# Both ends of a two-layer encoder kernel: parameter load, first weight pieces, clock warm-up, root table and stores

## The chip, the cores and the metric

The kernel runs on one core of one Trainium2 chip. The metric is the device time of one execution in microseconds (us). A core has TensorE (matmul, "PE" in the profile, its weight loads "PEld"), VectorE ("DVE"), ScalarE ("ACT"), GpSimd ("POOL") and SyncE ("SP"), which here only issues DMAs. A DMA is issued by an engine's queue (SPq, ACTq, POOLq) and carried out by 16 DMA engines that all queues share.

## The reference

`reference()` runs two layers over x, 512 tokens of 1024 channels. Cut to what matters:

```python
for l in range(DEPTH):                      # DEPTH = 2
    x = x + 0.5 * swiglu_ffn(rmsnorm(x, ffn1_norm[l]), ffn1_w_in[l], ffn1_w_out[l])
    h = rmsnorm(x, mix_norm[l])
    ...                                     # RWKV-7, gated linear attention, memory attention
    x = x + merged @ w_out[l]
    x = x + 0.5 * swiglu_ffn(rmsnorm(x, ffn2_norm[l]), ffn2_w_in[l], ffn2_w_out[l])
return rmsnorm(x, final_norm)

def rmsnorm(x, g):
    y = x * rsqrt(mean(x * x, axis=-1) + 1e-6)
    return y * g

def swiglu_ffn(h, w_in, w_out):             # 1024 -> 2 x 2816 -> 1024
    gate, up = split(h @ w_in, 2)
    return (silu(gate) * up) @ w_out
```

The change touches the start of the first layer's `ffn1` and the last `ffn2` together with the final `rmsnorm`.

## The kernel before

x is held transposed in eight tiles `x[k]` of 128 channels by 512 tokens (`T`). All products are float32 made from two-part operands: `split` writes a rounded part `hi` (ScalarE, a copy) and the remainder `lo` (VectorE, a subtraction), and `mm3` adds hi·hi, hi·lo and lo·hi in PSUM.

*Order of the work.* The program is recorded first: every call becomes an `Op` in a `Recorder`, with its dependences worked out from the areas that it reads and writes. `cost` gives every operation a duration, `run` plays the list through five engines and one DMA pipe, `urgency` works out backwards how late each may start, and `plan` repeats this six times and keeps the order with the earliest end. `issue` then emits that order, which is fixed on each engine. TensorE prefers the order of recording; the other engines take what is most urgent among what is ready.

*Front.* `setup` loads the parameter tile `par` (124 columns, among them the norm gains) through GpSimd's queue, runs `NWARM` = 9 products of a column of ones, whose result nobody reads, and loads x through SyncE. `ffn` then makes `xr` (the two parts of x times the norm gain, `raw_in`: tiles xrh and xrl; the eighth k is called xr), starts the sum of squares for the norm (`rstd`, tiles sq and sqa, a product with ones, a root, a reciprocal and a product with the unit matrix that spreads the result over the partitions), and computes the first four hidden tiles with plain products: `whole(j)`. The norm's factor `rs` is applied only to the result, so these products need not wait for it. `whole` loads the 1 MB of tile j in two pieces of 512 KB (k = 0 to 3 and 4 to 7; gate and up side by side), splits each, and makes 2 x 3 matmuls for every k. The split pieces `whi` and `wlo` have two buffers each, the raw piece `wraw` three. The other hidden tiles go through `seven`, a scheme of seven half-size products for four, with operands made in `blocks_in`; its loads use the ring `q`, and some of them are accumulated by GpSimd's DMAs. The memory's norm is interleaved into the first layer's down products (`aside`) and borrows two buffers of `q`.

*End.* The hidden tiles of the last `ffn` come in three blocks, each followed by its four down products (o = 0 to 3, two tiles of x each). Before the last block's down products a one-element Sqrt is recorded (`self.root`), which loads Sqrt's table into ScalarE; it reads slot 0 of the last pair of hidden tiles, written when the pair's even tile is done. `finish` squares x[0] to x[5] whole and sums them, then takes the two halves of the tokens in turn (the upper first): squares of x[6] and x[7], sums over the partitions by products with ones (in ps_f and ps_c), root, reciprocal, spreading by the unit matrix `cst`, and then for every k one VectorE product with the gain and the factor and one store of 128 KB on SyncE's queue: 16 stores.

Of the kernel before, what the change touches and what calls it, by code (L numbers as in the profile page):

```python
# [19 lines left out]
P = 128  # L20
T = 512
D = 1024
KD = 8
# [7 lines left out]
NWARM = 9  # L31
# [253 lines left out]
class Recorder:  # L285
# [65 lines left out]
    def cost(self, o, ins, outs, a, k):  # L351
# [32 lines left out]
        elif o.engine == "scalar":  # L384
# [11 lines left out]
        else:  # L396
# [3 lines left out]
            o.busy, o.took = max(440, o.pipe), o.pipe + 1450  # L400
# [33 lines left out]
    def run(self, late):  # L434
# [42 lines left out]
        while events:  # L477
# [22 lines left out]
            for e in touched:  # L500
# [21 lines left out]
                if o.pipe is not None:  # L522
                    dma = max(t + 400, dma) + o.pipe
                    o.took = dma - t + (1050 if e == "sync" else 2550)
# [15 lines left out]
    def urgency(self, order):  # L540
# [7 lines left out]
        for o in reversed(order):  # L548
            t = late.get(o, math.inf)
            for q in o.next:  # L550
                g = self.lag(o, q)
                took = o.took if o.pipe is None else o.pipe + (1450 if o.engine == "sync" else 2950)
# [41 lines left out]
class Net:  # L594
# [34 lines left out]
    def setup(self):  # L629
# [3 lines left out]
        nc.gpsimd.dma_start(out=self.par, in_=I["par"][0])  # L633
# [6 lines left out]
        self.x = [self.keep.tile([P, T], F32, name=f"x{k}", tag=f"x{k}") for k in range(KD)]  # L640
# [331 lines left out]
    def ffn(self, w_in, w_out, norm, aside=None, last=False):  # L972
# [3 lines left out]
        with ExitStack() as ctx:  # L976
# [7 lines left out]
            def whole(j):  # L984
                src = w_in[j]
                pp = self.big(), self.small("i")
                w = [self.piece(pool, self.load(src, c, c + 2 * T).rearrange("p (c t) -> p c t", c=2)) for c in (0, 2 * T)]
                for k in range(KD):
                    ks = slice(k % 4 * P, k % 4 * P + P)
                    for ps, (a, b) in zip(pp, w[k // 4]):  # L990
                        self.mm3(ps, (a[:, ks], b[:, ks]), xs[k], k == 0, k == KD - 1)
# [61 lines left out]
            def jobs():  # L1053
                for b, (j0, j1) in enumerate(BLOCKS):
# [4 lines left out]
                    if b == len(BLOCKS) - 1 and last:  # L1059
                        self.root = self.nrm.tile([P, 4], F32, name="rt", tag="rt", bufs=2)  # L1060
                        nc.scalar.activation(self.root[:, 0:1], Ms[b][n - 1][0][:, 0, 0:1].bitcast(F32), AF.Sqrt,
                                             bias=self.eps[:, 0:1], scale=0.0)
                    for o in range(4):
                        if aside is not None and b == 0 and o == 1:
                            aside(pool)
                        nc.part = "down"
# [724 lines left out]
    def finish(self, out):  # L1791

        nc = self.nc
        acc, sq = (self.keep.tile([P, 2, T], F32, name="sqa", tag=t) for t in ("kT", "vm"))
        rt = self.root
        for k in range(KD - 2):
            nc.scalar.activation(acc[:, int(k > 0)], self.x[k], AF.Square)
            if k:
                nc.vector.tensor_tensor(acc[:, 0], acc[:, 0], acc[:, 1], ALU.add)
        for i, hs in enumerate(HALVES[::-1]):  # L1800
            for k in range(2):
                nc.scalar.activation(sq[:, k, hs], self.x[KD - 2 + k][:, hs], AF.Square)
# [11 lines left out]
            for k in range(KD):  # L1814
# [79 lines left out]
```

## Time and profile before

| | |
|---|---|
| median of 3 runs | 2542.26 us (2540.98 to 2543.71) |
| profiled execution | 2542.58 us, of which the span is 2540.7 |
| busy, share of the span | PE 99%, PEld 89%, DVE 83%, ACT 58%, POOL 10% |
| chain that ended last | PE 86%, DVE 7%, DMA 3%, issue 2%, ACT 1% |
| TensorE without work, 0 to 50 us | 3.5 us |
| TensorE without work, 100 to 150 us | 4.0 us |
| DMA over the span | 358 MB, 141 GB/s on average |

"Busy" counts from the start of an engine's instruction to its end. The chain is followed back from the last instruction to what released it. In a row of the timeline the first two numbers are start and length in us, then come engine, line, operation, out<-in, and in square brackets how long the engine had been idle and what ended that. Nearly everything has line 316, since the calls are replayed from there, so instructions are told apart by their tiles. A row of a window table has the window, its length, the busy time and count for PE, PEld, DVE, ACT and POOL, the granted TensorE clock (1.00 is full speed), the busy share of the DMA engines and their GB/s. "DMA to landing" is the time from a DMA's issue until its data are there.

### The profile page before, as it was taken

Reading aid. Unit: us, or ns where it says so; the run is one execution under the profiler, and the core shown is the slowest. Engines: PE = TensorE matmul, PEld = TensorE weight load, DVE = VectorE, ACT = ScalarE, POOL = GpSimd, SP = SyncE. Lnnn points to the kernel's source line nnn. Section 1 sums busy time; section 2 is a strip of 40 time slices with the busy share of each in tenths; the row PEclk is TensorE's granted clock in tenths of the full one; section 3 lists DMA queues with packets and bytes.
Section 4 is the critical chain, followed back from the end, with each engine's and each line's share of the span. In section 5 each row is a group of like instructions: output and inputs, shape, how many; then the busy total and the mean of one; then the engine's idle time right before and its main releaser. Section 6 shows DMA issues by size and latency. Waiting matters only on the chain.

```text
span 2540.7 us, 47191 instructions
## 1 busy us (share of the span) xinstructions
PE 2506.8 (99%) x17630; PEld 2270.9 (89%) x17630; DVE 2099.7 (83%) x4218; ACT 1467.9 (58%) x2660; POOL 241.4 (10%) x363
## 2 busy tenths in 40 slices
PE   9999999999999999999999999999999999999998
PEld 8999988888888899999989999877887788899998
DVE  7988885778888689888889888766878877898877
ACT  6665666664544456565655656674745444565655
POOL 1111100000000001211101111000000000011110
PEclk9999999999999999999999999999999999999999
DMA  6787762322222556877558776523222225468773
GB/s 194 186 200 185 171 189 81 118 79 69 69 83 74 144 156 153 206 188 185 145 132 202 188 188 168 170 87 103 83 69 88 67 77 170 134 165 208 187 177 100
DMA packets 162884, 358.02 MB, mean 141 GB/s; under 512 B 18224, under 2 KB 37104, under 8 KB 162656
## 3 DMA queue, kind: packets, MB, share of 16 engines
q1 hardware_dynamic: 125760, 289.92, 37.0%
q0 software_dynamic: 36896, 65.09, 16.4%
q8 instruction: 139, 2.28, 0.4%
q14 instruction: 89, 0.73, 0.1%
HBM read 342.88 MB, written 12.06 MB: 140 GB/s over the span
## 4 chain that ended last, share of the span: by engine, by line
PE 86%; DVE 7%; DMA 3%; issue 2%; ACT 1%; SPq 0%; DVEq 0%; ACTq 0%; POOLq 0%
PE ps_b L316 41%; PE ps_i L316 25%; PE ps_f L316 10%; PE ps_c L316 9%; PE ps_y L316 2%; DVE wlo L316 1%; DMA q<-in_ffn_out_dram 1%; DVE x L316 1%; DMA mt<-in_mem_dram 1%; DVE lo L316 0%; ACT whi L316 0%; DMA q<-in_w_out_dram 0%; DMA wraw<-in_ffn_in_dram 0%; DMA wraw<-in_w_out_dram 0%; ACT hi L316 0%
## 5 line engine op out<-in xcount | busy, mean ns | idle before, releaser
L316 ACT ACTIVATE hi<-q 128x512 fp32r<-128x512 f32 (+3 forms) x384 | 289.2, 756 | 206.1 <-PE ps_i L316 67.6
L316 DVE TENSOR_TENSOR lo<-q,hi 128x512 fp32r<-128x512 f32 (+3 forms) x384 | 323.0, 843 | 44.6 <-ACT hi L316 44.3
L316 PE MATMUL ps_b<-xhi,whi 128*128 128x512 f32 (+1 forms) x880 | 353.7, 402 | 0.2 <-DVE rk_r L316 0.2
L316 PE MATMUL ps_b<-xlo,whi 128*128 128x512 f32 (+1 forms) x880 | 352.9, 401 | 0.1
L316 PE MATMUL ps_b<-xhi,wlo 128*128 128x512 f32 x864 | 347.1, 402 | 0.4 <-DVE wlo L316 0.3
L316 DVE TENSOR_TENSOR wlo<-wraw,whi 128x1024 fp32r<-128x1024 f32 (+1 forms) x172 | 183.8, 1069 | 74.7 <-ACT whi L316 70.5
L316 DVE TENSOR_TENSOR lo<-wraw,hi 128x1024 fp32r<-128x1024 f32 (+1 forms) x160 | 191.6, 1197 | 59.7 <-ACT hi L316 58.7
L316 ACT ACTIVATE whi<-wraw 128x1024 fp32r<-128x1024 f32 (+1 forms) x174 | 161.7, 929 | 129.6 <-PE ps_b L316 99.5
L316 ACT ACTIVATE hi<-wraw 128x1024 fp32r<-128x1024 f32 (+1 forms) x160 | 165.8, 1036 | 106.6 <-PE ps_i L316 41.2
L316 PEld LDWEIGHTS ps_b<-xlo,whi 128*128 128x128 f32 (+1 forms) x880 | 164.1, 187 | 35.6 <-DVE xlo L316 2.5
L316 PEld LDWEIGHTS ps_b<-xhi,whi 128*128 128x128 f32 (+1 forms) x880 | 164.4, 187 | 33.6 <-issue 1.2
L316 PEld LDWEIGHTS ps_b<-xhi,wlo 128*128 128x128 f32 x864 | 162.7, 188 | 32.5 <-DVE wlo L316 1.9
L316 PE MATMUL ps_i<-mh,hi 128*128 128x256 f32 x628 | 157.3, 283 | 8.0 <-DVE x L316 6.0
L316 PE MATMUL ps_i<-ml,hi 128*128 128x256 f32 x624 | 155.0, 281 | 0.0
L316 PE MATMUL ps_b<-xhi,hi 128*128 128x256 f32 x576 | 144.4, 283 | 0.0
L316 PE MATMUL ps_b<-xlo,hi 128*128 128x256 f32 x576 | 144.3, 283 | 0.0
L316 PEld LDWEIGHTS ps_i<-mh,hi 128*128 128x128 f32 x628 | 119.0, 190 | 10.1 <-ACT hi L316 3.8
L316 PEld LDWEIGHTS ps_i<-ml,hi 128*128 128x128 f32 x624 | 118.1, 190 | 0.0
L316 PEld LDWEIGHTS ps_b<-xhi,hi 128*128 128x128 f32 x576 | 110.5, 192 | 0.2
L316 PEld LDWEIGHTS ps_b<-xlo,hi 128*128 128x128 f32 x576 | 110.4, 192 | 0.1
L316 ACT ACT_TABLE_LOAD x73 | 93.7, 1283 | 15.9 <-DVE gc L316 10.8
L316 PE MATMUL ps_b<-ml,hi 128*128 128x256 f32 x416 | 101.9, 278 | 0.0
(415 smaller groups left out, 7011.2 us busy)
## 6 DMA issues: line engine op xcount, KB each, us to landing
wraw<-in_w_main_dram SPq DMA_DIRECT2D x108, 512.0 KB, 3.6
wraw<-in_ffn_in_dram SPq DMA_DIRECT2D x104, 512.0 KB, 4.5
q<-in_ffn_in_dram SPq DMA_DIRECT2D x144, 256.0 KB, 4.5
q<-in_ffn_in_dram POOLq DMA_DIRECT2D x72, 256.0 KB, 5.8
d<-in_ffn_in_dram SPq DMA_DIRECT2D x72, 256.0 KB, 4.3
wraw<-in_ffn_in_dram POOLq DMA_DIRECT2D x72, 256.0 KB, 5.4
wraw<-in_ffn_out_dram SPq DMA_DIRECT2D x32, 512.0 KB, 4.4
q<-in_ffn_out_dram SPq DMA_DIRECT2D x64, 256.0 KB, 3.7
```

The costliest lines, as they stand in the source:

```text
L316: return getattr(getattr(self.tc.nc, engine), what)(*(f(v) for v in a), **{n: f(v) for n, v in k.items()})
```

## The change

- `setup`: `par` of layer 0 is loaded by ScalarE's queue, and 12 products of ones run instead of 9. The planner learns the cost of a DMA on ScalarE's queue.
- `x` becomes one tile `xs` of 128 x 8 x 512, of which x[k] are views.
- `whole(0)` of the first `ffn` loads four pieces of two k (256 KB) instead of two pieces of four k; all other hidden tiles keep pieces of four k. Load, split and products are now recorded piece by piece.
- The one-element Sqrt is recorded between the down products o = 1 and o = 2 of the last block and reads slot 6 of the last pair, written with the last odd tile's upper half, after its Silu.
- `finish`: x[0] to x[5] are multiplied by the gain early, after their squares. In each half, x[0..2] and x[3..5] then take one product with the factor each (three tiles at once) and one store of 384 KB, on SyncE's and on ScalarE's queue; x[6] and x[7] take the former product and a store of 128 KB each, one on each queue: 8 stores.

```diff
-NWARM = 9
+NWARM = 12
...
-        nc.gpsimd.dma_start(out=self.par, in_=I["par"][0])
+        nc.scalar.dma_start(out=self.par, in_=I["par"][0])
...
-        self.x = [self.keep.tile([P, T], F32, name=f"x{k}", tag=f"x{k}") for k in range(KD)]
+        self.xs = self.keep.tile([P, KD, T], F32, name="x", tag="x")
+        self.x = [self.xs[:, k, :] for k in range(KD)]
...
-                w = [self.piece(pool, self.load(src, c, c + 2 * T).rearrange("p (c t) -> p c t", c=2)) for c in (0, 2 * T)]
-                for k in range(KD):
-                    ks = slice(k % 4 * P, k % 4 * P + P)
-                    for ps, (a, b) in zip(pp, w[k // 4]):
-                        self.mm3(ps, (a[:, ks], b[:, ks]), xs[k], k == 0, k == KD - 1)
+                n = fine if j == 0 else 4
+                wide = src.rearrange("p (h c t) -> p h c t", h=2, c=2)
+                for k0 in range(0, KD, n):
+                    raw = self.wp.tile([P, 2, n * P], F32, name="wraw", tag="wraw", bufs=3)
+                    t0 = k0 % 4 * P
+                    nc.sync.dma_start(out=raw, in_=wide[:, k0 // 4, :, t0:t0 + n * P])
+                    w = self.piece(pool, raw)
+                    for k in range(k0, k0 + n):
+                        ks = slice((k - k0) * P, (k - k0 + 1) * P)
+                        for ps, (a, b) in zip(pp, w):
+                            self.mm3(ps, (a[:, ks], b[:, ks]), xs[k], k == 0, k == KD - 1)
...
-                    if b == len(BLOCKS) - 1 and last:
-                        self.root = self.nrm.tile([P, 4], F32, name="rt", tag="rt", bufs=2)
-                        nc.scalar.activation(self.root[:, 0:1], Ms[b][n - 1][0][:, 0, 0:1].bitcast(F32), AF.Sqrt,
-                                             bias=self.eps[:, 0:1], scale=0.0)
                     for o in range(4):
...
+                        if b == len(BLOCKS) - 1 and last and o == 2:
+                            self.root = self.nrm.tile([P, 4], F32, name="rt", tag="rt", bufs=2)
+                            nc.scalar.activation(self.root[:, 0:1], Ms[b][n - 1][0][:, 6, 0:1].bitcast(F32), AF.Sqrt,
+                                                 bias=self.eps[:, 0:1], scale=0.0)
...
-        for k in range(KD - 2):
+        early = KD - 2
+        for k in range(early):
             nc.scalar.activation(acc[:, int(k > 0)], self.x[k], AF.Square)
             if k:
                 nc.vector.tensor_tensor(acc[:, 0], acc[:, 0], acc[:, 1], ALU.add)
+            nc.vector.tensor_scalar(self.x[k], self.x[k], self.pcol("final_norm", k), None, ALU.mult)
+        rows = out.rearrange("(k p) t -> p k t", p=P)
...
-            for k in range(KD):
-                nc.vector.scalar_tensor_tensor(self.x[k][:, hs], self.x[k][:, hs], self.pcol("final_norm", k), ps[:, :H],
+            for k0, k1, queue in ((0, 3, nc.sync), (3, early, nc.scalar)):
+                nc.vector.tensor_tensor(x[:, k0:k1, hs], x[:, k0:k1, hs],
+                                        ps[:, :H].unsqueeze(1).to_broadcast([P, k1 - k0, H]), ALU.mult)
+                queue.dma_start(out=rows[:, k0:k1, hs], in_=x[:, k0:k1, hs])
+            for k, queue in ((KD - 2, nc.sync), (KD - 1, nc.scalar)):
+                nc.vector.scalar_tensor_tensor(x[:, k, hs], x[:, k, hs], self.pcol("final_norm", k), ps[:, :H],
                                                ALU.mult, ALU.mult)
-                nc.sync.dma_start(out=out[k * P:(k + 1) * P, hs], in_=self.x[k][:, hs])
+                queue.dma_start(out=rows[:, k, hs], in_=x[:, k, hs])
...
-            self.ffn(self.I["ffn1_in"][l], self.I["ffn1_out"][l], "ffn1_norm", self.layer_params)
+            self.ffn(self.I["ffn1_in"][l], self.I["ffn1_out"][l], "ffn1_norm", self.layer_params, fine=4 if l else 2)
```

More of the change, by code (lines that the diff above doesn't have):

```diff
@@ L383, in cost @@
             o.busy = max(o.took - 80, 60)
-        elif o.engine == "scalar":
+        elif o.engine == "scalar" and o.what != "dma_start":
             n = out.n
@@ L399, in cost @@
             o.pipe = size / 230
-            o.busy, o.took = max(440, o.pipe), o.pipe + 1450
+            o.busy, o.took = 440 if o.engine == "scalar" else max(440, o.pipe), o.pipe + 1450
     HOP, SLACK = 34, 60
@@ L523, in run @@
                     dma = max(t + 400, dma) + o.pipe
-                    o.took = dma - t + (1050 if e == "sync" else 2550)
+                    o.took = dma - t + (2550 if e == "gpsimd" else 1050)
                 if e == "tensor":
@@ L551, in urgency @@
                 g = self.lag(o, q)
-                took = o.took if o.pipe is None else o.pipe + (1450 if o.engine == "sync" else 2950)
+                took = o.took if o.pipe is None else o.pipe + (2950 if o.engine == "gpsimd" else 1450)
                 t = min(t, late[q] - (o.busy if g is None else took + g))
@@ L970, in outputs, with ffn @@
         return evict
-    def ffn(self, w_in, w_out, norm, aside=None, last=False):
+    def ffn(self, w_in, w_out, norm, aside=None, last=False, fine=4):
         nc, l = self.nc, self.l
@@ L1791, in finish @@
     def finish(self, out):
-        nc = self.nc
+        nc, x = self.nc, self.xs
         acc, sq = (self.keep.tile([P, 2, T], F32, name="sqa", tag=t) for t in ("kT", "vm"))
         rt = self.root
-        for k in range(KD - 2):
+        early = KD - 2
+        for k in range(early):
             nc.scalar.activation(acc[:, int(k > 0)], self.x[k], AF.Square)
@@ L1799, in finish @@
                 nc.vector.tensor_tensor(acc[:, 0], acc[:, 0], acc[:, 1], ALU.add)
+            nc.vector.tensor_scalar(self.x[k], self.x[k], self.pcol("final_norm", k), None, ALU.mult)
+        rows = out.rearrange("(k p) t -> p k t", p=P)
         for i, hs in enumerate(HALVES[::-1]):
-            for k in range(2):
-                nc.scalar.activation(sq[:, k, hs], self.x[KD - 2 + k][:, hs], AF.Square)
+            for k in range(early, KD):
+                nc.scalar.activation(sq[:, k - early, hs], self.x[k][:, hs], AF.Square)
             ps, r = self.small("fc"[i]), rt[:, 2 * i:2 * i + 2]
```

## The prediction, made before the changed kernel was run

> **What bounds the kernel now.** I read the page's head and its chain first, then the two ends of the span in order of time, then windows.
>
> ```profile
> span 2540.7 us, 47191 instructions
> ...
> PE 2506.8 (99%) x17630; PEld 2270.9 (89%) x17630; DVE 2099.7 (83%) x4218; ACT 1467.9 (58%) x2660; POOL 241.4 (10%) x363
> ...
> PE 86%; DVE 7%; DMA 3%; issue 2%; ACT 1%; SPq 0%; DVEq 0%; ACTq 0%; POOLq 0%
> ```
>
> TensorE is busy for 99% of the span and carries 86% of the chain that ended last. A change that leaves the matmuls alone can win only where TensorE stands still or runs slowly: at the front, at the end, or in one of the few waits between. The front, in order of time (start, length, engine):
>
> ```profile
> 0.94 4.21 PE L316 MATMUL ps_y<-one 128*128 128x128 f32 x18 [0.94 <-DVE eps L316]
> 1.20 1.37 SPq L316 DMA_DIRECT2D x<-in_x_dram  x3
> 1.29 0.70 POOL L316 DMA_DIRECT2D par<-in_par_dram  x1 [0.83 <-POOLq L1876]
> ...
> 5.19 1.06 ACT L316 ACTIVATE hi<-wraw 128x1024 fp32r<-128x1024 f32 x1 [3.15 <-DMA wraw<-in_ffn_in_dram]
> ...
> 6.28 1.23 DVE L316 TENSOR_TENSOR lo<-wraw,hi 128x1024 fp32r<-128x1024 f32 x1 [5.33 <-ACT hi L316]
> 6.67 1.32 ACT L316 ACTIVATE xrh<-x,par 128x512 fp32r<-128x512 f32 x2
> ...
> 7.43 0.50 PE L316 MATMUL ps_b<-xrh,hi 128*128 128x512 f32 x1 [2.28 <-ACT xrh L316]
> ...
> DMA to landing us min/median/max: 4.8/6.6/6.8
> ...
> DMA to landing us min/median/max: 5.2/5.2/5.2
> ...
> 7.43:22.28 14.85, 14.57 (x56) 11.53 (x56) 12.18 (x21) 9.94 (x17) 0.00 (x0) 0.89 0.72 265
> 8.45:11.92 3.47, 3.47 (x8) 2.73 (x9) 3.47 (x5) 3.47 (x7) 0.00 (x0) 0.52 1.05 401
> ...
> 0.76 4.41 DMA wraw<-in_ffn_in_dram
> ...
> 35.01 0.69 PE ps_b L316 x3
> ```
>
> The first two columns of a window row are its bounds and length; PEclk and the DMA share stand near its end; the two landing lines are those of x and of par. The run on ones, nine products in 18 passes, ends at 5.15, and the first real matmul starts at 7.43. It waits for xrh, which needs the weights (0.76 + 4.41 = 5.17), x0 (1.20 + 4.8 = 6.00) and par (1.29 + 5.2 = 6.49). After the gap of 2.28 us the granted clock averages 0.52 from 8.45 to 11.92. A settled matmul takes 0.69/3 = 0.229 us. The 56 between 7.43 and 22.28 would take 12.8 of the 14.85 us, so the front behaves like a full-speed start at 7.43 + 2.05 = 9.48. Of the 2.05 us the slow clock costs 3.47 - 8 x 0.229 = 1.64.
>
> The end, from the last eviction of x on:
>
> ```profile
> 2526.20 1.39 PE L316 MATMUL ps_f<-one,sqa 128*128 128x1 f32 x12
> ...
> 2526.86 0.42 ACT L316 ACTIVATE sqa<-x 128x256 f32<-128x256 f32 x1 [0.66 <-DVE x L316]
> 2527.29 1.28 ACT L316 ACT_TABLE_LOAD   x1
> ...
> 2527.45 0.58 PE L316 MATMUL ps_c<-one,sqa 128*128 128x1 f32 x4
> 2528.59 0.26 ACT L316 ACTIVATE rt<-ps_f,eps 128x2 f32<-128x2 f32 x1
> ...
> 2528.88 0.32 DVE L316 RECIPROCAL rt<-rt 128x2 f32<-128x2 f32 x2 [2.06 <-ACT rt L316]
> ...
> 2529.10 0.71 PE L316 MATMUL ps_f<-cst,rt 128*128 128x128 f32 x4 [1.06 <-DVE rt L316]
> ...
> 2529.85 3.22 DVE L316 SCALAR_TENSOR_TENSOR x<-x,par,ps_f 128x256 f32<-128x256 f32 x8 [0.65 <-PE ps_f L316]
> 2530.36 7.72 SPq L316 DMA_DIRECT2D out_dram<-x  x16
> ...
> 2531.00:2539.00 8.00, 0.00 (x0) 0.00 (x0) 5.21 (x14) 0.00 (x0) 0.00 (x0) 0.50 0.79 262
> ...
> 2539.00:2539.50 0.50, 0.00 (x0) 0.00 (x0) 0.00 (x0) 0.00 (x0) 0.00 (x0) 0.50 0.04 10
> ```
>
> A table load of 1.28 us stands between the last square and the root. Then VectorE makes a 128x256 product every 0.40 us, SyncE needs 7.72/16 = 0.48 us for each store of 128 KB, and bytes flow at 262 GB/s with the DMA engines 0.79 busy until just after 2539.0. 131 KB in 0.48 us are 272 GB/s: the one queue's issuing sets this rate, not the engines.
>
> **The change, part by part.**
>
> *Start of real work.* par leaves GpSimd's queue for ScalarE's, which is free at 0.76: it starts at least 0.5 us earlier. ScalarE's first work is at 5.19, which hides the issue and, if the issue stands ahead of it, the delayed first table load; GpSimd's next work comes long after. The first weight piece shrinks from 512 to 256 KB.
>
> ```profile
> 3.00:15.00 12.00, 9.44 (x35) 7.41 (x34) 8.72 (x15) 9.80 (x16) 0.00 (x0) 0.86 1.03 373
> ...
> L316 ACT ACTIVATE hi<-q 128x512 fp32r<-128x512 f32 x224 | 141.4, 631 | 111.0 <-PE ps_i L316 56.2 <-DVE q L316 19.1 <-PE ps_c L316 11.2
> ...
> 54.07 0.69 DVE L316 TENSOR_TENSOR lo<-q,hi 128x512 fp32r<-128x512 f32 x1
> ```
>
> At 373 GB/s the 262 KB less that lie ahead of x0 are 0.70 us: pieces at 4.47, x0 at 5.30. Splitting a half piece costs ScalarE 0.63 instead of 1.06, done at 5.1; xrh then takes 0.71 of the 1.32 us for two, so the operands are there at 6.06 (with the 0.05 from its end, 7.38, to the matmul at 7.43). The longer run on ones is 12/9 x 4.21 = 5.61 us and ends at 6.55 if its passes stay as slow. TensorE's order is fixed, so the later counts: 6.55, and between 6.06 and 6.55 if the clock rises during the run. I take 6.55, so 0.49 us of the extra products lie on the path and the rest beside the loads. The gap that let the clock fall is gone, so the 1.64 us go too; I keep the 0.41 us of early waits on xrl that remain of the 2.05. New effective start 6.96, gain 9.48 - 6.96 = 2.52. SyncE issues two loads more, 1.37/3 = 0.46 us each, which is less than the 0.70 us that such a piece takes to flow.
>
> *What is late next: VectorE.*
>
> ```profile
> 19.02 0.69 DVE L316 TENSOR_TENSOR sqa<-sqa,sq 128x512 f32<-128x512 f32 x1
> ...
> 22.51 0.95 PE L316 MATMUL ps_f<-one,sqa 128*128 128x1 f32 x8
> ...
> 27.26 0.69 DVE L316 COPY xt<-ps_f 128x512 f32<-128x512 f32 x1 [2.17 <-PE ps_f L316]
> ...
> 87.12:110.00 22.88, 22.69 (x191) 22.46 (x190) 22.88 (x48) 14.19 (x29) 2.58 (x3) 1.00 0.65 157
> ```
>
> It works without a gap from 6.28 to 19.71 on the lo parts and the sum of squares, which TensorE reduces at 22.51: 2.8 us of slack. It will start about 1.1 us earlier (5.1 against 6.28 less the hand-over), but two whole pieces become four, 2 x (2 x 0.69 - 1.23) = 0.30 us more, and it will wait some 0.3 us for xrh. So it ends near 19.2, and TensorE, 2.5 us early, wants it at 20.0: it fits, with 0.8 us left. I take the extra 0.30 off all the same, since half pieces use up the two buffers of whi and wlo after two steps of k instead of four: the front gains 2.2 us. Its low end is 0.9 (the clock falls anyway, 2.52 - 1.64), its high end 3.0 (start at 6.06).
>
> *Does it reach the end?* From 27.26 to 110 VectorE has no idle time (22.88 of 22.88 us in the quoted row), and then comes the one real hole:
>
> ```profile
> 110.00:130.00 20.00, 15.97 (x136) 15.61 (x135) 15.88 (x34) 9.06 (x16) 4.31 (x5) 1.00 0.89 224
> ...
> 102.72 4.05 DMA q<-in_ffn_out_dram
> ...
> 107.33 6.11 DMA q<-in_ffn_out_dram
> ```
>
> TensorE idles 4.03 us there, waiting for a load that VectorE's progress released and a second one that GpSimd adds on top. The stretch on VectorE begins with a copy at 27.26 that waits for TensorE's reduction, so all of it slides with TensorE. The instruction order is made anew, because costs and work at the front changed; I put this at 0 with 2 us either way, half the hole. Layer 1, ffn2 and the later hidden tiles load the same 512 KB pieces as before and cost nothing: their cover is TensorE's own backlog.
>
> *Root table.* The early root reads slot 6 of the last pair, which is written after the last Silu, so Sqrt's table stays loaded and the 1.28 us at 2527.29 go. Then the chain is limited by TensorE's sums: those of the high half end at 2526.20 + 1.39 = 2527.59. Root 0.06 later, 0.26 long, reciprocal 0.29 after the root's start, TensorE 0.22 after that, VectorE 0.75 after that: 2527.65 + 0.29 + 0.22 + 0.75 = 2528.91 against 2529.85: 0.94 us. The load itself moves under the down products; if it held those up it would cost its 1.28 us.
>
> *Stores.*
>
> ```profile
> L316 DVE TENSOR_TENSOR lo<-wraw,hi 128x768 fp32r<-128x768 f32 x16 | 15.3, 956 | 2.7 <-ACT hi L316 2.1
> ...
> L316 DVE TENSOR_SCALAR pr<-pr,mx 128x256 f32<-128x256 f32 x32 | 10.1, 350 | 0.5
> ...
> 2520.00:2530.00 10.00, 8.94 (x79) 8.85 (x77) 5.07 (x14) 5.12 (x11) 0.00 (x0) 1.00 0.00 0
> ```
>
> A product over three tiles (768 elements) takes about 0.96 us, so the first store is ready 0.96 instead of 0.42 us after the start, 0.54 later. After that each half brings its 512 KB of work in 2 x 0.96 + 2 x 0.40 = 2.7 us at most, against 3.22, and eight issues share two queues, so neither VectorE nor issuing limits. What is left is the DMA engines: 262/0.79 = 332 GB/s. 2097 KB then flow in 6.3 us. They flowed until about 2539.06, so from 2531.2 (2097 KB at 266 GB/s back from there); now from 2531.2 - 0.94 + 0.54 = 2530.8 to 2537.1. The end as a whole gains 1.95 us, root table included. If the rate stayed at 262 it would gain 0.3; at the front's 373 it would gain 2.7. ScalarE's stores wait for VectorE; the second half's root, if it stood behind one, is covered by the 3.2 us that the first megabyte takes to flow. The six products with final_norm (128x512, up to 2 x 0.35 us each, 4.2 in all) hide in VectorE's idle half of the last 10 us and behind TensorE before that; without cover the last two would cost 1.4.
>
> The Trainium skill, "DMA: Bandwidth & Descriptors", section "Issuing engines are not separate DMA queues", says that issuing from several engines saves only the issue time, usually little. Here the 0.48 us per store is that time and it is the bound, so the page and the row agree on a gain up to the engines' own rate; were issuing not the bound, the page would give the 262 GB/s case.
>
> **Sum.** 2.2 + 1.95 = 4.15 us off the profiled 2542.58 (span 2540.7 and 1.9 around it): 2538.4. The profiled run lies 0.3 above the median of the three, 2542.26, so 2538.1.
>
> **Rivals.**
>
> *Front eaten.* The clock falls again, or VectorE's in-order waits for free whi buffers hold TensorE: front 0.9, end 1.95, 2539.4 or, with the front at 0, 2540.3. For it: the gap that remains is not seen before it is run. Against: the run on ones now reaches past the operands. The Trainium skill, "TensorE: Matmul & The Clock Gate", section "What's actually happening", says that the clock is judged over free-running windows of about 3.4 us. The slow stretch of 3.47 us agrees. By it a kernel that starts at another phase could still run one such window slowly, which is this rival.
>
> *Stores bound by the engines.* At 262 GB/s the end gives 0.3: 2542.26 - 2.2 - 0.3 = 2539.8. For it: packets of 1 KB as before; against: share 0.79.
>
> *The table load does not go.* Square may not be in Sqrt's table; in the stretches that I read no Square follows Sqrt's load before another load. Then 0.94 comes back: 2539.0. The Trainium skill, "ScalarE: Activation LUTs", section "Table sets: the hidden batching unit", lists relu, copy, identity and abs as present in every set and does not name square.
>
> *More than the sum.* Front 3.0 and end 2.7 (start at 6.06, stores at 373 GB/s): 2536.6, and 2535.6 if the hole at 110 shrinks by 1. For it: most of the loads at the front already flow at that rate. Against: it needs every bound to fall well.
>
> *Slower.* Half pieces starve the front: four hand-overs (third and fourth piece, both pieces of the next tile) wait for a buffer and expose their splits, 2 x (0.63 + 0.69) + 2 x (1.06 + 1.23) = 7.2 us, 2538.1 + 7.2 = 2545.3, slower by 3. It decides once more than 4.15 of the 7.2 us are exposed. Against: between release and need lie two steps of k, 12 x 0.229 = 2.7 us, over 1.3 or 2.3 needed.
>
> **How the numbers follow.** Forecast as summed 0.45; more than the sum 0.26; front eaten 0.10; stores bound 0.08; table stays 0.04; slower 0.07. What a measurement of this kernel can tell from no change is about 0.2%, 5.1 us, so the forecast itself counts as within it. Faster by more, under 2537.2: 0.28, the second case and a little of the first. Slower by more, over 2547.3: 0.03, the far part of the last case. Within: 0.69. The range runs from 2535.8 (second case) to 2541.8 (front eaten with 1.5 of the 2 us lost in the middle).
>
> **What would show it.** Right: first real matmul near 6.5 with the clock at 1.00 from there; the reduction on ones near 20; no table load after the last square; first product near 0.94 us sooner after the last eviction; over 300 GB/s at the end. Wrong: a slow clock after 8, TensorE idle before 20, a copy at 27 that did not move, or a larger hole near 110.

## The result and the profile after

The changed kernel takes 2532.34 us (median of 7 runs, 2529.51 to 2535.00) against 2540.98 for the kernel before in the same comparison: ratio 0.9967, 95% interval 0.9958 to 0.9977, so 8.4 us faster (5.8 to 10.7). Measured again with other kernels (e14 below) it took 2531.72, ratio 0.9970 (0.9958 to 0.9982), 7.6 us. The forecast was 4.15 us. The profiled execution took 2534.68 us, 7.9 less than that of the kernel before.

The head of its page and its chain:

```profile
span 2532.7 us, 47197 instructions
PE 2506.4 (99%) x17636; PEld 2270.3 (90%) x17636; DVE 2100.5 (83%) x4218; ACT 1466.9 (58%) x2660; POOL 241.2 (10%) x362
...
PE 85%; DVE 8%; DMA 3%; ACT 2%; issue 2%; SPq 0%; DVEq 0%; ACTq 0%; POOLq 0%
```

TensorE's busy time is the same as before (2506.4 against 2506.8 us): all of the gain is time in which it stood still or ran slowly. The front in order of time, columns as in the prediction:

```profile
0.75 0.41 ACTq L316 DMA_DIRECT2D par<-in_par_dram  x1
0.76 0.38 SPq L316 DMA_DIRECT2D x<-in_x_dram  x1
...
0.94 5.49 PE L316 MATMUL ps_y<-one 128*128 128x128 f32 x24 [0.94 <-DVE one L316]
...
3.72 1.28 ACT L316 ACT_TABLE_LOAD   x1 [3.72 <-DMA x<-in_x_dram]
...
5.01 0.72 ACT L316 ACTIVATE xrh<-x,par 128x512 fp32r<-128x512 f32 x1
...
6.16 0.61 ACT L316 ACTIVATE hi<-wraw 128x512 fp32r<-128x512 f32 x1
...
6.83 0.50 PE L316 MATMUL ps_b<-xrh,hi 128*128 128x512 f32 x1 [0.40 <-ACT hi L316]
...
20.59 0.95 PE L316 MATMUL ps_f<-one,sqa 128*128 128x1 f32 x8
```

The run on ones ends at 6.43, the first real matmul starts at 6.83, and the reduction on ones has come from 22.51 to 20.59. New is a table load at 3.72, after x0 has landed. In the kernel before it ran at the start:

```profile
0.76 1.28 ACT L316 ACT_TABLE_LOAD   x1 [0.76 <-PEq L1876]
```

SyncE also issues x0 ahead of the first weights now (0.76); before, it stood behind them (1.20). Three windows of the changed kernel:

```profile
8.45:11.92 3.47, 3.47 (x16) 2.56 (x15) 3.47 (x7) 3.47 (x8) 0.00 (x0) 1.00 0.97 341
...
110.00:130.00 20.00, 18.13 (x152) 17.62 (x151) 17.80 (x34) 11.07 (x18) 3.48 (x4) 1.00 0.94 221
...
2525.00:2530.50 5.50, 0.00 (x0) 0.00 (x0) 3.14 (x6) 0.00 (x0) 0.00 (x0) 0.55 1.01 341
```

In the first, 16 matmuls at clock 1.00 stand where 8 at 0.52 stood. In the second TensorE makes 152 matmuls where it made 136: the hole has shrunk from 4.0 to 1.9 us. In the third the stores flow at 341 GB/s with the DMA engines full, where they flowed at 262 with 0.79. The chain of work through the hole (start, length, what):

```profile
100.75 3.83 DMA q<-in_ffn_out_dram
...
105.13 4.74 DMA q<-in_ffn_out_dram
...
109.95 0.64 ACT hi L316
```

The second line is GpSimd's accumulating load. It starts 2.20 us earlier than before (105.13 against 107.33), of which the front explains about 2, and it also takes 4.74 instead of 6.11 us. The end:

```profile
2492.65 1.28 ACT L316 ACT_TABLE_LOAD   x1
...
2500.56 0.64 ACT L316 ACTIVATE sqa<-x 128x512 f32<-128x512 f32 x1
...
2520.53 0.42 DVE L316 SCALAR_TENSOR_TENSOR x<-ps_i,x 128x256 f32<-128x256 f32 x1 [0.66 <-PE ps_i L316]
2520.99 0.42 ACT L316 ACTIVATE sqa<-x 128x256 f32<-128x256 f32 x1 [0.66 <-DVE x L316]
...
2521.76 0.26 ACT L316 ACTIVATE rt<-ps_f,eps 128x2 f32<-128x2 f32 x1 [0.36 <-PE ps_f L316]
...
2523.02 1.82 DVE L316 TENSOR_TENSOR x<-x,ps_f 128x768 f32<-128x768 f32 x2 [0.36 <-PE ps_f L316]
2524.01 4.10 SPq L316 DMA_DIRECT2D out_dram<-x  x4
...
2524.87 3.81 ACTq L316 DMA_DIRECT2D out_dram<-x  x4
```

The table load at 2492.65 is the last one: the squares run in Sqrt's table set, and nothing stands between the last square and the root but TensorE's sums. In the kernel before, the last eviction of x started at 2526.40 and the first product at 2529.85, 3.45 us later; here it is 2523.02 - 2520.53 = 2.49. From that eviction to the end of the span it was 2540.7 - 2526.40 = 14.30 and is 2532.7 - 2520.53 = 12.17: the end gains 2.13.

**Where the 7.9 us of the two profiled runs lie.** The table loads of the norms and roots serve as marks along the span. Of the kernel before and of the changed kernel:

```profile
29.04 1.28 ACT L316 ACT_TABLE_LOAD   x1
140.32 1.28 ACT L316 ACT_TABLE_LOAD   x1
...
2210.26 1.28 ACT L316 ACT_TABLE_LOAD   x1
```

```profile
26.89 1.28 ACT L316 ACT_TABLE_LOAD   x1
136.48 1.28 ACT L316 ACT_TABLE_LOAD   x1
...
2203.92 1.28 ACT L316 ACT_TABLE_LOAD   x1
```

2.15 us are won by the first mark, 1.69 more by the second, 2.50 between the second and the third; 0.5 is lost from there to the last eviction of x, and 2.13 are won after it. The third stretch, apart from its first microseconds, has the same order on every engine in both kernels. So there are two things to explain: the hole, which the forecast had put at 0, and the 2.50.

### The profile page after: what moved, and what is told of

It is laid out like the page before. It is cut to its first block, busy times and chain, and to the rows that moved or that the text cites. A ratio compares the mean times of both kernels' runs of the same rounds, so it can differ in the third digit from the quotient of the medians.

```text
span 2532.7 us, 47197 instructions
## 1 busy us (share of the span) xinstructions
PE 2506.4 (99%) x17636; PEld 2270.3 (90%) x17636; DVE 2100.5 (83%) x4218; ACT 1466.9 (58%) x2660; POOL 241.2 (10%) x362
## 4 chain that ended last, share of the span: by engine, by line
PE 85%; DVE 8%; DMA 3%; ACT 2%; issue 2%; SPq 0%; DVEq 0%; ACTq 0%; POOLq 0%
PE ps_b L316 40%; PE ps_i L316 25%; PE ps_f L316 10%; PE ps_c L316 9%; PE ps_y L316 1%; DVE wlo L316 1%; DVE lo L316 1%; DVE x L316 1%; DMA q<-in_ffn_out_dram 1%; ACT whi L316 1%; DMA wraw<-in_w_out_dram 0%; DVE ml L316 0%; DMA wraw<-in_ffn_in_dram 0%; ACT hi L316 0%; DMA q<-in_ffn_in_dram 0%
## 5 line engine op out<-in xcount | busy, mean ns | idle before, releaser
L316 DVE TENSOR_TENSOR lo<-wraw,hi 128x1024 fp32r<-128x1024 f32 (+2 forms) x162 | 191.5, 1182 | 48.5 <-ACT hi L316 46.5
L316 ACT ACTIVATE hi<-wraw 128x1024 fp32r<-128x1024 f32 (+2 forms) x162 | 166.3, 1026 | 106.1 <-PE ps_i L316 41.0
L316 DVE TENSOR_TENSOR q<-q 128x512 f32<-128x512 f32 (+1 forms) x128 | 85.5, 668 | 22.9 <-DMA q<-in_ffn_in_dram 19.0
```

The lines of the kernel that those rows point to most:

```text
L316: return getattr(getattr(self.tc.nc, engine), what)(*(f(v) for v in a), **{n: f(v) for n, v in k.items()})
```

## The experiments

Theory A: the order that the planner made anew is worth 2 to 3 us at the hole. Its rivals are B (all work merely arrives earlier), C (scatter of the middle) and D (the end is worth more). Each comparison has its own runs of the kernel before.

| | time, us (runs) | ratio to before, 95% interval |
|---|---|---|
| e1 new front | 2533.46 (9) | 0.9973, 0.9963 to 0.9983 |
| e2 new end | 2537.32 (11) | 0.9986, 0.9977 to 0.9995 |
| e3 new front, old order | 2537.54 (11) | 0.9989, 0.9980 to 0.9998 |
| e4 old front, new order | 2538.60 (11) | 0.9987, 0.9977 to 0.9997 |
| e5 two instructions moved | 2537.51 (11) | 0.9993, 0.9984 to 1.0002 |
| e6 early table load | 2532.75 (7) | 0.9975, 0.9964 to 0.9986 |
| e7 nine products on ones | 2536.24 (11) | 0.9992, 0.9982 to 1.0002 |
| e8 one queue | 2532.56 (11) | 0.9974, 0.9965 to 0.9983 |
| e9 two instructions back | 2532.28 (6) | 0.9970, 0.9958 to 0.9981 |
| e10 square first | 2532.17 (9) | 0.9971, 0.9961 to 0.9981 |
| e11 whole pieces | 2535.42 (1) | |
| e12 par by GpSimd | 2531.76 (1) | |
| e13 all but the front | 2535.54 (11) | 0.9982, 0.9973 to 0.9991 |
| e14 changed kernel again | 2531.72 (6) | 0.9970, 0.9958 to 0.9982 |
| e15 old root | 2532.60 (6) | 0.9972, 0.9960 to 0.9983 |

What the traces say at the two places, for those that the argument needs. "Reduction" is the start of the reduction on ones, "29 to 140" the time between the first two marks, "accumulating" the time of GpSimd's load of q that starts between 103 and 109 us:

| kernel | reduction | 29 to 140 | matmuls, 110 to 130 | accumulating |
|---|---|---|---|---|
| before | 22.51 | 111.28 | 136 | 6.1 |
| e2 | 23.38 | 111.22 | 137 | 6.0 |
| e3 | 20.60 | 111.88 | 130 | 6.6 |
| e11 | 22.91 | 110.57 | 143 | 6.0 |
| changed | 20.59 | 109.59 | 152 | 4.7 |
| e1 | 20.64 | 109.63 | 152 | 5.7 |
| e4 | 23.21 | 109.47 | 158 | 4.1 |
| e14 | 20.71 | 110.03 | 151 | 4.2 |
| e5 | 23.53 | 108.46 | 164 | 4.3 |
| e13 | 22.38 | 108.35 | 164 | 4.3 |
| e9 | 19.62 | 109.84 | 158 | 4.3 |
| e8 | 19.81 | 110.05 | 153 | 6.0 |
| e15 | 19.66 | 109.00 | 163 | 6.4 |

**e1: the new front alone** (root and `finish` as before), against the kernel before:

```diff
-NWARM = 9
+NWARM = 12
-nc.gpsimd.dma_start(out=self.par, in_=I["par"][0])
+nc.scalar.dma_start(out=self.par, in_=I["par"][0])
...
+n = fine if j == 0 else 4                              # and whole() by pieces, fine = 2 in layer 0
```

> The new front alone; the root table and the stores stand as before. The planner makes its order anew here too, so the weights of the second tile come ahead of the second output load at 100 to 105 us, as in the changed kernel. Theory A (the re-made order): 1.9 us from the front and 2 to 3 us from a smaller hole at 100 to 130 us, so 4 to 5 us faster than before, near 2536.5, with TensorE idle about 2 instead of 4 us between 110 and 130. Theory B (only the earlier arrival of all work counts, the order does not): 1.9 us, near 2539. Theory C (the 8 us are half scatter of the middle of the kernel): anything between, with the shift against before wandering by 3 us between 150 and 2450 us.

6.9 us faster. The reduction is at 20.64, the hole shrinks as in the changed kernel. That is A, or B; more than the 4 to 5 us that A allowed.

**e2: the new end alone,** against the kernel before:

```diff
-if b == len(BLOCKS) - 1 and last:                      # root, slot 0
+if b == len(BLOCKS) - 1 and last and o == 2:           # root, slot 6
...
+for k0, k1, queue in ((0, 3, nc.sync), (3, early, nc.scalar)):   # and the rest of finish()
```

> The new end alone (root table in another place, wide products, eight stores on two queues); front and order up to the end as before. All theories: the end gives 2.1 us (root 0.96, rest 1.17), near 2539; the hole at 110 to 130 us stays at 4 us of idle TensorE. Theory D (the end is worth more than its trace shows): 4 us or more, under 2537. What the shift does between 150 and 2450 us, where nothing differs from before, shows how far the middle scatters by itself.

3.6 us faster (1.3 to 5.8), so D has no support. The order up to the end is that of the kernel before, and the stretch with the hole takes as long (29 to 140: 111.22 us). It also has marks at 29.89 and 2209.02, where the kernel before has 29.04 and 2210.26: the same work in the same order took 2.1 us less. This is the scatter of theory C, and it accounts for the 2.50 us of the third stretch: from the second mark to the third the profiled run of the kernel before is 0.7 (e15) to 4.4 us (e14) longer than that of each of the other sixteen, and its 2542.58 lies 2.3 above the median of the 31 runs beside e1 to e4, 2540.31. The hole of e2 has something that the profile of before did not show. Its wait and two windows:

```profile
116.11 0.55 PE L316 MATMUL ps_i<-mh,hi 128*128 128x256 f32 x1 [2.84 <-DVE x L316]
...
116.00:120.00 4.00, 3.90 (x22) 3.93 (x23) 3.38 (x7) 2.51 (x4) 0.86 (x1) 0.62 0.83 223
110.00:130.00 20.00, 17.16 (x137) 17.00 (x136) 16.02 (x32) 8.82 (x17) 3.65 (x5) 0.91 0.87 216
```

After the wait of 2.84 us the granted clock averages 0.62 for 4 us: 22 matmuls instead of 36. e3's hole shows the same (0.91 over the 20 us); those of before and e11 do not, though TensorE waited longer there (3.23 and 3.07 us). The Trainium skill, "TensorE: Matmul & The Clock Gate", section "What's actually happening", has the clock judged over free-running windows of about 3.4 us; a hole of this length that costs a slow window in two of four profiles agrees with it.

**e3 and e4: front and order taken apart.** From 60 us of the plan on, e3 takes the order of the kernel before, e4 that of e1:

```diff
+FRONT[0] = False                     # e4: True
+other = Net(ctx, tc, ins); other.run(out); there = other.nc.plan()
+FRONT[0] = True                      # e4: False
...
-net.nc.issue(net.nc.plan())
+net.nc.issue(hybrid(net.nc, net.nc.plan(), other.nc, there))
```

> The new front, the old end, and from 60 us of the plan on every engine's order exactly as in the kernel before. Theory A (order): the front's 1.9 us and no more, near 2539; TensorE still idles about 4 us between 110 and 130, and the weights of the second tile are still issued behind the second output load. Theory B (earlier arrival): the same 4 to 5 us as the new front with its own order, the hole shrinks all the same.

> The old front and the old end, with every engine's order from 60 us of the plan on taken from the kernel with the new front. Theory A (order): 2 to 3 us faster than before, near 2538.5, TensorE idle about 2 us between 110 and 130, first reduction on ones at 22.5 us as before. Theory B (earlier arrival): no change, near 2541, hole of 4 us.

2.8 us faster for e3 and 3.3 for e4, each about half of e1's 6.9. In e3 everything arrives 2 us earlier and the hole stays: TensorE waits 2.99 us, a slow window follows, and the 130 matmuls are the fewest of all. The accumulating load is at its slowest:

```profile
104.47 6.57 DMA q<-in_ffn_out_dram
...
113.29 0.36 PE L316 MATMUL ps_i<-mh,hi 128*128 128x256 f32 x1 [2.99 <-DVE x L316]
```

```profile
110.00:130.00 20.00, 17.01 (x130) 16.66 (x129) 16.95 (x35) 9.76 (x17) 4.32 (x5) 0.91 0.85 218
```

In e4 nothing arrives earlier and the hole shrinks all the same (158 matmuls). B falls, A stands: the re-made order by itself is worth 1.8 us in the trace of e4 (111.28 against 109.47 from the first mark to the second). The times have intervals of 0.5 to 5.1 us for e3 and 0.8 to 5.8 for e4 and do not tell the two apart; the traces do.

**e5 and e9: which part of the order.** e5 is the kernel before with two instructions moved at 102 us of the plan:

```diff
+ahead(pick("vector", "tensor_tensor", "q", ("wraw", "wraw"), 123), pick("vector", "tensor_tensor", "lo", ("q", "hi"), 371))
+ahead(pick("dma", "dma_start", "wraw", (), 438), pick("dma", "dma_start", "q", (), 366))
```

> The kernel before with two instructions moved, nothing else: at 102 us VectorE's difference q<-wraw stands ahead of two splits, and with it SyncE's load of a 512 KB weight piece stands ahead of the second load of q instead of behind it. Theory A1 (in the old order that piece is issued just ahead of GpSimd's accumulating load and shares the engines with it): the accumulating load lands in 4 to 5.8 us instead of 6.1 to 6.6, ScalarE's wait for it at 113 shrinks, TensorE idles 1 to 2 us instead of 3 to 4 between 110 and 130, and no slow clock follows: 2 to 3 us faster than before, near 2538. Theory A2 (the hole follows from the other moves of the new order, the splits of the later pieces): same as before, hole of 3 to 4 us.

The accumulating load of e5, and TensorE's wait behind it, first in the kernel before, then in e5:

```profile
107.95 4.29 DMA q<-in_ffn_out_dram
```

```profile
115.69 0.36 PE L316 MATMUL ps_i<-mh,hi 128*128 128x256 f32 x1 [3.23 <-DVE x L316]
```

```profile
114.49 0.36 PE L316 MATMUL ps_i<-mh,hi 128*128 128x256 f32 x1 [0.62 <-DVE x L316]
```

The accumulating load takes 4.29 us, and TensorE's wait for x, 3.23 us before, is 0.62. That is A1: the two instructions are enough, and e13, which has them too, shows it again (4.3 us, 164 matmuls). The time moved by 1.8 us only and could be 0 (interval -0.5 to 4.1), and the reduction of this profile is 1 us later than that of the profile before (23.53 against 22.51). Its first real matmul is only 0.20 us later, since xrh waited for par; the rest is the pace of the matmuls:

```profile
7.63 0.79 PE L316 MATMUL ps_b<-xrh,hi 128*128 128x512 f32 x1 [2.48 <-ACT xrh L316]
...
12.17 0.63 PE L316 MATMUL ps_i<-xrh,hi 128*128 128x512 f32 x1
...
8.45:11.92 3.47, 3.30 (x8) 2.32 (x8) 3.47 (x6) 3.47 (x7) 0.00 (x0) 1.00 1.05 403
```

From the first real matmul to 12.6 us each takes 0.6 us or more, and most start 0.43 us apart, 8 in the window where the changed kernel has 16. The window's clock reads 1.00 all the same, so in this stretch that column does not tell and the pace has to be read. e2 and e4 run like this too, 12 and 13 matmuls from their first one (7.70 and 7.49) to 13 us; in before and e13 it is 8, from 8.4 us on. The old front thus comes in two forms, with the reduction at 22.4 to 22.5 or at 23.2 to 23.5. e9 does the reverse in the changed kernel:

```diff
+back = pick("vector", "tensor_tensor", "q", ("wraw", "wraw"), 123)
+for n in (371, 370):
+    ahead(pick("vector", "tensor_tensor", "lo", ("q", "hi"), n), back)
+ahead(pick("dma", "dma_start", "q", (), 366), pick("dma", "dma_start", "wraw", (), 438))
```

> The changed kernel with the same two instructions put back: VectorE's difference q<-wraw behind the two splits at 102 us, and SyncE's 512 KB weight piece behind the second load of q. All else stays in the new order. Theory A1 (that piece right ahead of the accumulating load is what makes the hole): the accumulating load takes 6 us or more again, TensorE idles 3 us or more between 108 and 118 us, 2 to 3 us slower than the changed kernel, near 2535. Theory A2 (the other moves of the new order carry it too): the hole stays at about 1 us there, same as the changed kernel, 2532.4.

No change (2532.28), accumulating load 4.3 us, no long wait, and 109.84 us from the first mark to the second, as in the changed kernel and e14. So the two instructions suffice to close the hole in the old order and are not what keeps it closed in the new one, where splits of later pieces have moved as well. Why the accumulating load is slow is less clear. Where the 512 KB piece left SyncE 0.2 to 1.0 us ahead of it (before, e2, e3, e11) it took 6.0 to 6.6 us. Where the 256 KB load of q was SyncE's last and left less than 0.6 us ahead of it or with it (e1, e7, e8, e15), it took 5.5 to 6.4. Where q had a lead of 0.7 to 1.8 us (changed, e4, e5, e6, e10, e12, e13, e14), or the piece one of 1.3 (e9), it took 4.1 to 4.7. So in all seventeen profiles the slow ones start close behind another load. That the two share the DMA engines fits this, but it is argued, not shown: while the load was under way the engines were busy for 0.78 of the time in before and for 0.91 in e5, where it was faster. The hole was short in e1, e7, e8 and e15 all the same, so what keeps it short in the new order, beside this load, stays open.

**e6, e10 and e12: the table load at the front.** In the changed kernel the load waits for x0. The built program's list of ScalarE shows why (order and waits, no times), first of the changed kernel, then of e10:

```
DMA par   TABLE_LOAD [waits DMAHW1]   xrh<-x,par [waits DMAHW0]
DMA par   TABLE_LOAD                  sqa<-x [waits DMAHW1]     xrh<-x,par [waits DMAHW0]
```

DMAHW1 tells that x0 has landed, DMAHW0 that par has. xrh needs both; one of its two waits stands at the table load ahead of it. The planner puts now xrh, now the square first: xrh in the changed kernel, e1, e3, e5, e6, e7, e11 and e14, the square in the kernel before and in e2, e4, e8, e9, e12, e13 and e15. The front of e8, e9 and e15 is that of the changed kernel without an edit, so the source does not fix which comes out; their reductions lie at 19.62 to 19.81, 0.8 to 1.0 us sooner than the changed kernel's, and their times contain that. e6 adds a tiny Square behind the issue of par, e10 puts the square first, e12 leaves par on GpSimd's queue.

```diff
+net.nc.scalar.activation(net.eps[:, 2:3], net.one, AF.Square)       # e6
```

```diff
+order.remove(sqa); order.insert(order.index(xrh), sqa)              # e10
```

```diff
-nc.scalar.dma_start(out=self.par, in_=I["par"][0])                  # e12
+nc.gpsimd.dma_start(out=self.par, in_=I["par"][0])
```

> The changed kernel with one tiny Square on ScalarE right behind the issue of par, so that its table load runs near 1.2 us and not behind the wait for x0 (3.72 to 5.00 us in the changed kernel). Theory E (the late table load is on the front's path): xrh near 3.8, the first split of weights as soon as they land, first real matmul at the end of the run on ones or near 6.4 instead of 6.83, about 0.4 us less than the changed kernel, near 2532. Theory F (the path is the landing of the first half piece): first matmul stays at 6.8, no gain.

> The changed kernel with ScalarE's first square of x0 ahead of xrh, so that the step behind the table load needs one wait and not two and the load runs at 1.2 us. Theory E: first real matmul near 5.8 to 6.0 instead of 6.83, reduction on ones near 19.8 instead of 20.6, 0.8 us less than the changed kernel, near 2531.5. Theory F (VectorE becomes late instead, so that TensorE gives it back before the reduction): reduction at 20.6, no gain.

> The changed kernel with par back on GpSimd's queue. One look for the front: par lands near 6.5 instead of 3.8, so if it is on the path the first xrh starts at 6.5 and the first real matmul near 7.3; if not, the first real matmul stays at or under 6.8, since the table load runs at 0.76 here.

The front of e10:

```profile
1.20 1.28 ACT L316 ACT_TABLE_LOAD   x1 [1.20 <-PEq L1890]
...
5.63 0.50 PE L316 MATMUL ps_b<-xrh,hi 128*128 128x512 f32 x1
...
19.76 0.95 PE L316 MATMUL ps_f<-one,sqa 128*128 128x1 f32 x8
```

The load runs at 1.19 to 1.20 us in e6 and e10; the first matmul comes at 6.01 and 5.63 and the reduction at 20.22 and 19.76, 0.4 and 0.8 us sooner than in the changed kernel. That is E. The times, 2532.75 and 2532.17, cannot tell 0.8 us; e10 is the better front by its trace and no faster by its time. e12 has its load at 0.75 and par at 4.8 (not the expected 6.5): first matmul 6.10, reduction 20.55 (one execution). Moving par thus gains 0.8 us where the square is first, and in the changed kernel the late table load takes that back, by one profile each.

**e7 and e11: what keeps the clock up.** Both against the changed kernel; in e11 the planner goes back to the old order at the hole.

```diff
-NWARM = 12                                             # e7
+NWARM = 9
```

```diff
-self.ffn(..., self.layer_params, fine=4 if l else 2)   # e11: whole pieces
+self.ffn(..., self.layer_params)
```

> The changed kernel with nine products on ones instead of twelve; order otherwise the same. The run on ones ends at 4.5 to 5.2 us, the first real matmul stays at 6.83 since it waits for ScalarE. Theory P (the gap of 1.7 to 2.3 us lets the clock fall, as before): matmuls at half clock for about 3.5 us after 8 us, reduction on ones 1.6 us later than in the changed kernel, 2534. Theory Q (what counts is only the earlier start): no slow clock, same as the changed kernel, 2532.4.

> The changed kernel with whole 512 KB first pieces instead of halves; par on ScalarE's queue and twelve products on ones stay, and the planner falls back to the old order around 100 us. One look for the front: if the half pieces carry the earlier start, the first split starts near 5.2 as before and the first real matmul near 7.4 with the run on ones ended at 5.7 to 6.4, and the reduction on ones lies at 21 or later; if they do nothing, the first real matmul stays at 6.8. The old order again: TensorE idle 3 us or more at 113 to 117 us.

Timeline and window of e7, then of e11:

```profile
6.83 0.50 PE L316 MATMUL ps_b<-xrh,hi 128*128 128x512 f32 x1 [1.76 <-ACT hi L316]
```

```profile
8.45:11.92 3.47, 3.47 (x10) 2.75 (x9) 3.47 (x7) 3.47 (x8) 0.00 (x0) 0.54 0.97 365
```

```profile
7.64 0.51 PE L316 MATMUL ps_b<-xrh,hi 128*128 128x512 f32 x1 [1.64 <-ACT xrh L316]
```

```profile
8.45:11.92 3.47, 2.99 (x7) 2.42 (x8) 3.47 (x6) 3.47 (x7) 0.00 (x0) 0.55 1.05 406
```

In e7 the first real matmul starts at the same 6.83, but after a gap of 1.76 us, and the clock is 0.54 where it was 1.00: reduction 21.80, 1.2 us later. That is P. (Its time is 3.5 us above those of e6 and e8, which ran beside it, with single runs up to 2544.62; that is more than the trace explains, and why stays open.) e11's gap of 1.64 does the same, and its first split starts at 5.90, when its weights land: the half pieces bring the earlier start and the longer run closes the gap; either alone leaves the slow stretch, by one profile each. With whole pieces the planner also puts x0 behind the first weights again, so the size of the pieces and the order of the loads are not told apart. The gaps of 0.40 (changed), 1.13 (e3) and 1.14 (e1) were followed by no slow clock.

**e8 and e15: the two parts of the end.** e8 issues all eight stores by SyncE; e15 records the early Sqrt at its old place.

```diff
-for k0, k1, queue in ((0, 3, nc.sync), (3, early, nc.scalar)):       # e8
+for k0, k1, queue in ((0, 3, nc.sync), (3, early, nc.sync)):
...
-for k, queue in ((KD - 2, nc.sync), (KD - 1, nc.scalar)):
+for k, queue in ((KD - 2, nc.sync), (KD - 1, nc.sync)):
```

> The changed kernel with all eight stores issued by SyncE. In the changed kernel the two queues spend 4.10 and 3.81 us on four stores each, side by side. Theory X (eight issues instead of sixteen were enough): the end stays within 0.3 us of the changed kernel's 9.68 us from the first product to the end of the span. Theory Y (issue time goes with bytes, so one queue is again the bound): eight issues take about 7.9 us one behind the other, the end takes 11 us or more, 1 to 2 us slower than the changed kernel, near 2534.

```profile
2521.17 1.82 DVE L316 TENSOR_TENSOR x<-x,ps_f 128x768 f32<-128x768 f32 x2 [0.36 <-PE ps_f L316]
2522.15 5.74 SPq L316 DMA_DIRECT2D out_dram<-x  x8
...
2523.00:2528.50 5.50, 0.00 (x0) 0.00 (x0) 3.28 (x6) 0.00 (x0) 0.00 (x0) 0.50 1.00 336
```

From the first product to the end of the span (2530.8) 9.63 us, as with two queues (9.68): X. One queue issues the eight stores in 5.74 us, 0.72 each, which is less than the data take to flow, and the engines are full; so the second queue does nothing here, and the gain came from fewer, larger stores. The Trainium skill, "DMA: Bandwidth & Descriptors", section "Issuing engines are not separate DMA queues", says that issuing from several engines saves only the time of issuing; e8 agrees.

```diff
+if b == len(BLOCKS) - 1 and last:                      # e15: ahead of the four down products, slot 0
-if b == len(BLOCKS) - 1 and last and o == 2:
```

> The changed kernel with the early root back in its old place, ahead of the last Silu. By the trace the table load returns behind the last square and costs 0.9 to 1.0 us between the last eviction of x and the first product: 1 us slower than the changed kernel, near 2533.3. If instead the down products pay for the new place of the load, no difference.

```profile
2521.11 1.28 ACT L316 ACT_TABLE_LOAD   x1
...
2522.92 1.23 PE L316 MATMUL ps_f<-cst,rt 128*128 128x128 f32 x4 [1.06 <-DVE rt L316]
...
2524.18 1.82 DVE L316 TENSOR_TENSOR x<-x,ps_f 128x768 f32<-128x768 f32 x2 [1.16 <-PE ps_f L316]
```

The table load is back behind the last square, and the first product comes 3.96 us after the last eviction (2520.22), 1.47 more than in the changed kernel: 0.96 is the load (root at 2.19 against 1.23 us after the eviction), the rest TensorE's four spreading products, which took 1.23 instead of 0.71 us in this profile, at a granted clock of 0.50 instead of 1.00. The time, 2532.60 against 2531.72 for e14, agrees but does not show it; the front of e15 is 1.0 us better than that of e14.

**e13 and e14: do the parts add up?** e14 is the changed kernel unaltered; e13 is e2 with the two instructions of e5:

```diff
-net.nc.issue(net.nc.plan())
+net.nc.issue(moved(net.nc, net.nc.plan()))             # the two ahead() lines of e5
```

> The change without its front: old front, new end, and only the two moved instructions at 102 us of the new order. If the parts add up by their traces (hole 1.9 to 2.8, end 2.1): 4.0 to 4.9 us faster than before, near 2535.5, and 2.7 us slower than the changed kernel. If the front is worth more in time than its trace shows (as the new front alone, 6.9 us faster, might say): no more than 2 us faster than before and 5 us slower than the changed kernel.

> The changed kernel once more, beside the others on the same chip. By its first 7 runs 2532.3; if the sum of the parts by their traces holds (front 2.7, hole 1.9, end 2.1), 6.7 us faster than before; if there is something more, 8.4 us as in the first runs.

e13 is 4.6 us faster than before (2.3 to 6.9), where hole and end by their traces gave 4.0 to 4.9. The medians of e13 and e14 lie 3.8 us apart, with an uncertainty of some 2 us by the spread of their 11 and 6 runs: that is the front. By the traces it is 2.4: the reductions of the five kernels with the old front (before, e2, e4, e5, e13) lie at 22.38 to 23.53, mean 23.00, those with the changed kernel's front (changed, e1, e3, e14) at 20.59 to 20.71. Parts by trace: 2.4 + 1.9 + 2.1 = 6.4 us. The slow window behind the old hole (14 matmuls in e2, at 4.00/37 us each 1.5 us) is not to be added: over the four profiles with the old hole, two with such a window and two without, the stretch from 29 to 140 averages 111.24 us, as long as in the profile before. The sum lies within the intervals of e14 (4.6 to 10.7 us) and of the first comparison (5.8 to 10.7), towards their low ends; the 1 to 2 us by which the times exceed the parts may be real or scatter.

## Why the prediction missed

- *Start of real work*: the run on ones (ends at 6.43, 6.55 forecast) and the clock (1.00) came out as forecast, the path of the operands did not. The prediction had x0 land at 5.30, behind the first weights; the new order loads it first, and it is there by 3.72. It also took the delayed table load for hidden behind ScalarE's free time; but the load waits for x0 and then costs 1.28 us on the path, and a square stands ahead of the split, so the first matmul is at 6.83 where the operands alone were to be ready at 6.06. Two errors of opposite sign are left in the front's gain, so that its size came out near is partly luck.
- *What is late next: VectorE*: right. The reduction came 1.92 us earlier against that profile and 2.4 against the mean of the five old fronts, 2.2 forecast; TensorE was without work for 1.4 us in the first 50, 3.5 before.
- *Does it reach the end?* This is the step that failed. It does reach the end, but the term for the order made anew, put "at 0 with 2 us either way", measured a gain of 1.9 us by the marks: 111.28 us from the first to the second before, 109.38 on average over ten kernels with the new order (1.2 to 2.9 us less). The prediction saw the hole, the late load and the accumulating load behind it, and then took the middle of a range where the planner's order had a definite effect. The prediction also read the old front off one execution, and a cheap one: its reduction at 22.51 lies near the low end of 22.38 to 23.53, since its slow stretch was the short one.
- *Root table*: 0.96 measured, 0.94 forecast. The rival that Square is not in Sqrt's table fell: no load follows the one at 2492.65.
- *Stores*: 341 GB/s, 332 forecast; the end as a whole gains 2.13, 1.95 forecast. It counted on two queues so that issuing would not limit; eight issues do not need the second one (e8).
- *Sum*: the base was a median of three, 2542.26; beside the changed kernel the kernel before took 2540.98, and in the later comparisons 2539.05 to 2540.33. So 1.3 of the 5.8 us between 2538.1 and 2532.34 are the base, and the rest is gain: 8.4 us where 4.15 were counted. The order accounts for 1.9 us of that difference, front and end for 0.2 each by their traces; for the 2 us that remain (1.2 by e14) no trace shows a place.
- The rivals *Front eaten*, *Stores bound by the engines* (262 GB/s) and *Slower* did not occur. *More than the sum* named the hole as a possible extra of 1 us, and was still short.

## What to carry to other kernels

Where an order is planned by machine, a small edit at one end re-deals the instructions near every tight place downstream: take the new order of the loads ahead of each known hole before calling the effect zero. A run of idle products is worth its length only if it reaches close to the first real product (here a gap of 1.14 us was short enough and one of 1.64 was not), and an earlier operand is worth it only if the gap behind the run closes too. And a base time for a forecast of 0.2% needs more than three runs.

## What the runs showed of the hardware that was not expected

- A wait of an instruction can come to stand at the table load ahead of it: with xrh first the load ran at 3.72 instead of 1.20 us, and the front lost 0.8 us.
- Gaps of 1.64 to 2.44 us on TensorE in the first 8 us were followed by a clock of 0.52 to 0.55 over 3.47 us (e11, e7, before, e13), gaps of up to 1.14 us were not. With the gaps of 2.34 to 2.55 us in e2, e4 and e5 the clock column reads 1.00, but the matmuls start 0.43 us apart until about 13 us: read the pace too. A wait of 2.8 to 3.2 us at 113 us was followed by a slow window in two of four profiles.
- Square runs in Sqrt's table set. The Trainium skill, "ScalarE: Activation LUTs", section "Table sets: the hidden batching unit", does not list it among those in every set; here ten squares follow Sqrt's load at 2492.65 without another one.
- Eight stores of 2.1 MB together keep the DMA engines full from one queue as well as from two (336 GB/s with a share of 1.00, 341 with 1.01).
